# Fourier units of a hybrid GLA/FNet step: 388 columns in one product, added at eviction

## The chip, the core and the metric

One core of one Trainium2 chip runs the whole program. The metric is the device time of one execution in microseconds (us), as the median of several runs. A profile is one execution taken by the hardware profiler; its span runs from the first to the last instruction.

The engines are TensorE (PE, with its weight loads as PEld), VectorE (DVE), ScalarE (ACT), GpSimd (POOL) and SyncE (SP), which here issues nearly all DMA transfers. Each executes its own instructions in order; they meet at semaphores.

## The reference

One layer of a diffusion backbone, on 128 context and 256 latent tokens (T = 384 columns everywhere), with 2048 channels:

```
mod = silu(cond) @ w_ada + b_ada            # six shifts, scales and gates
h = rmsnorm(x) * (1 + sc1) + sh1
proj = h @ w_in                             # GLA q, k, v, output gate, decay factors, Fourier channels
o = bidirectional gated linear attention, normalised, times silu(gate)
f = real part of the 2-D DFT of the Fourier channels over (positions, group channels), 4 groups of 256
g_a, g_b = sigmoid(h @ w_gate + b_gate)
merged = g_a * (o @ w_br_gla) + g_b * (f @ w_br_four)
x = x + ga1 * rmsnorm(merged @ w_out)
x = x + ga2 * rmsnorm(swiglu_ffn(rmsnorm(x) * (1 + sc2) + sh2))
```

Everything is float32. The part that the change touches is `f @ w_br_four`, with its gate. The real DFT is symmetric over positions: with n positions only n/2 + 1 are computed, 65 for the context and 129 for the latent tokens, 194 in all (`HT`), once as a cosine part and once as a sine part. Their sum gives one half of the positions, their difference, read backwards, the other.

## The kernel before, in words

Channels lie on the 128 partitions and tokens along the columns. A float32 matrix is split into a high part (rounded to `float32r`, which TensorE takes in one pass) and a low part (what is left), and a product is three TensorE instructions: high by high, high weight by low data, low weight by high data (`gemm`, L253 to L260). The data are split once. The weights come from memory as slabs of 128 x 1024 and are split on the way.

The weights have one order, written out by hand (`srcs`, L147 to L188). `grab` (L244) takes the slab that is due and at once starts the preparation of a later one (`push`): a transfer into one of two `raw` buffers (L196, on SP's queue), for a slab of `w_br_four` a fold on VectorE (L205 and L206, a sum and a difference of halves), a cast to the high part on ScalarE (L224), and the subtraction of the low part on VectorE (L225). Three slabs are ready or being made while one is used; `whi` and `wlo` have four buffers each. A Fourier slab's cast and subtraction are put off until the unit's output has been written in program order (`hold`, `settle`). PE, ACT, DVE and POOL execute in the order of the program text (`manual_schedule`, L129).

The stages: the modulation of the first sub-layer with the value projection; query and key; the gates (32 projections) with the attention beside them; the Fourier projection (L888 to L904: eight projections, with the DFT over channels and positions beside them, `dft`, L822); the mixing stage (L958 to L986); the output projection (L1020 on); the FFN.

The mixing stage goes through `mix_order` (L155 to L158): O0, then seven rounds of one O product and two Fourier units (O1, unit 0, unit 1, O2, unit 2, unit 3, ...), then A0, unit 14, A1, unit 15, A2 to A15. An O product (`proj` with `gcol`, L926) uses two slabs of `w_in`, 48 products of 384 columns; its eviction is a SiLU on ScalarE (L931, after a table load), three transposes (L929), a product on VectorE (L932), a cast (L283) and a subtraction (L284). An A product uses one slab of `w_br_gla`. A Fourier unit (`four`, L935) uses one slab of `w_br_four`: for the cosine part `eT` and the sine part `dT` of the data it runs `gemm` over four blocks of 128 channels, 12 products of 194 columns each, and one Nyquist product (L943). Both parts accumulate side by side in one PSUM bank (`pf`, from the pool `psm`, three buffers). ScalarE copies the sine part to `d` (L946; tag `fd`, one buffer), VectorE writes sums and differences to `y` in four pieces (L950, L951) and multiplies by the gate (L954), SP writes `y` to memory (L955). `gate_of` (L909) loads the gates ahead and applies the sigmoid on ScalarE. A second PSUM pool, `pss` (tag "side", five buffers), holds transposes and the products beside the main ones.

The modulation of the later sub-layers (`ada_rest`, L519) is spread over the stages: a step is a 512 KB transfer (L525) and two operations on VectorE of 128 x 1024 (L528 for the first block, L530 for the others); after 16 of them come an empty step, a reduction on TensorE (L538) and, with the next half's first block, two transposes (L547) and small VectorE operations (L552 on). Half a projection, or an A product, is a chance for a step; `paced` (L271) uses the share `rate[0]` of the chances: 1.0 in the gate stage, 0.7 in the Fourier projection, 0.25 in the mixing stage, 0.15 from A0 on, 0.6 in the output projection.

Of the kernel before, what the change touches and what calls it, by code (L numbers as in the profile page):

```python
# [11 lines left out]
F32 = mybir.dt.float32  # L12
F32R = mybir.dt.float32r
# [7 lines left out]
P = 128  # L21
# [4 lines left out]
T = TC + TL  # L26
# [22 lines left out]
HT = HC + HL  # L49
# [47 lines left out]
def tile_step(ctx: ExitStack, tc: tile.TileContext, a, o):  # L97
    nc = tc.nc
    PE, ACT, DVE, POOL, SP = nc.tensor, nc.scalar, nc.vector, nc.gpsimd, nc.sync
# [3 lines left out]
    actp = ctx.enter_context(tc.tile_pool(name="actp", bufs=1))  # L103
# [129 lines left out]
    def settle():  # L233
        if half_done:
            half_done.pop()()

    def push(at=None, eng=DVE, hold=False):
        load()
        split(at, eng, hold)

    def take():
        return ready.pop(0)

    def grab(hold=False):  # L244
        w = take()
        push(hold=hold)
        return w
# [5 lines left out]
    def gemm(dst, w, x, kts, n=P, n0=0, k0=0, first=True, last=True):  # L253

        for k in range(kts):
            for j, (wi, xi) in enumerate(((0, 0), (0, 1), (1, 0))):
                PE.matmul(  # L257
                    dst, w[wi][:, k * n + n0 : k * n + n0 + P], x[xi][:, k0 + k, :],
                    start=first and k == 0 and j == 0, stop=last and k == kts - 1 and j == 2,
                )  # L260
# [21 lines left out]
    def split_act(hi, lo, src):  # L282
        ACT.copy(hi, src)  # L283
        DVE.tensor_sub(lo, src, hi.bitcast(F32))  # L284
# [29 lines left out]
    psm = ctx.enter_context(tc.tile_pool(name="psm", bufs=3, space=PSUM))  # L314
    pss = ctx.enter_context(tc.tile_pool(name="pss", bufs=5, space=PSUM))
    with ExitStack() as s:
# [89 lines left out]
        def xprod(u, kb, w):  # L406
            def mm():
                for j, (x_, w_) in enumerate(passes(w)):
                    PE.matmul(px, w_[:, u * P : (u + 1) * P], hT[x_][:, kb, :], start=j == 0, stop=j == 2)  # L409

            return mm, lambda dst=None: flush(xacc[u], kb == 0, dst)
# [92 lines left out]
        for t in range(3):  # L504
            vprod(KT - 1, prev[0], range(3), (t,))
            if t < XU:
                mm, fl = xprod(t, KT - 1, prev[1])
# [59 lines left out]
    rate = [1.0]  # L567
# [235 lines left out]
    with ExitStack() as s:  # L803
        pc = s.enter_context(tc.tile_pool(name="pc", bufs=1))
# [3 lines left out]
        SP.dma_start(cd, a["consts"][:, b0:NC])  # L808
        oT = alloc_r("B", "o")

        cl = actp.tile([P, 13 * HT], F32R, tag="C_lo", name="edT").rearrange("p (n t) -> p n t", t=HT)
        eT, dT = (cl[:, 0:4], cl[:, 4:8]), (cl[:, 8:12], pc.tile([P, 4, HT], F32R, name="dlo"))
        pnr = cl[:, 12]
        fs = {}
        nyq = pc.tile([P, 3, P], F32, name="nyq")
        POOL.memset(nyq, 0.0)
# [2 lines left out]
        wn = pc.tile([P, D], F32R, name="wn")  # L819
        done = [0]  # L820

        def dft():  # L822


            def left(dst, stat, m):

                for lat, base, n in ((0, C_CT - b0, HC), (1, C_LT - b0, HL)):
                    for k in range(1 + lat):
                        c0 = base + (m * (1 + lat) + k) * n
                        PE.matmul(  # L830
                            dst[:, HC * lat : HC * lat + n], stat(lat + k), cd[:, c0 : c0 + n],
                            start=k == 0, stop=k == lat,
                        )

            for g in range(4):
                while done[0] < 2 * g + 2:
                    yield
                yield
                xc = pc.tile([P, 3, 2, 2, P], F32, tag="xc", name="xc")
                for t in range(3):  # L840
                    px = pss.tile([P, 257], F32, tag="side", name="px")
                    ts = slice(t * P, (t + 1) * P)
                    e, d = fs[g][:, 0, ts], fs[g][:, 1, ts]
                    PE.matmul(px, d, cd[:, 129:386], start=True, stop=False)  # L844
                    PE.matmul(px[:, 0:129], e, cd[:, 0:129], start=False, stop=True)

                    for m, c0 in enumerate((0, 129)):
                        ACT.copy(xc[:, t, m], px[:, c0 : c0 + P].unsqueeze(1).to_broadcast([P, 2, P]))
                    ACT.copy(nyq[:, t, g : g + 65 : 32], px[:, 128:129].to_broadcast([P, 3]))
                yield  # L850
                off = (P - 32 * g) % P
                rot = xc.rearrange("p t m r c -> p t m (r c)")
                for m, x in enumerate((eT, dT)):
                    pp = pss.tile([P, HT], F32, tag="side", name="pp")
                    left(pp, lambda k: rot[:, k, m, off : off + P], m)
                    split_act(x[0][:, g, :], x[1][:, g, :], pp)
                yield
            pn = pss.tile([P, HT], F32, tag="side", name="pn")
            left(pn, lambda k: nyq[:, k, :], 0)
            ACT.copy(pnr, pn)  # L860
            DVE.tensor_sub(pnr[64:96], pn[64:96], pnr[64:96].bitcast(F32))
            yield

        def nyq_weights(h):

            n = D // 2
            wr = pc.tile([P, n], F32, tag="ws", name="wr")
            POOL.memset(wr, 0.0)
            for g in range(4):
                src = a["w_br_four"][8 * h : 8 * h + 8, 32 * g : 32 * g + 1, (2 * g + 1) * P : (2 * g + 2) * P]  # L870
                for j in range(3):
                    r = 32 * j + g
                    SP.dma_start(wr[r : r + 1, :].rearrange("p (i c) -> p i c", c=P), src.rearrange("i p c -> p i c"))
            yield
            w = wn[:, n * h : n * h + n]
            ACT.copy(w, wr)
            DVE.tensor_sub(w[32:64], wr[32:64], w[32:64].bitcast(F32))
            yield

        df = dft()  # L880

        def side():
# [4 lines left out]

        sd = side()  # L888
        nw = (u for h in range(2) for u in nyq_weights(h))
        rate[0] = 0.7  # L890
        for i in range(8):
            def fo(p, i=i):
                if i % 2 == 0:
# [40 lines left out]

        def four(i):  # L935

            pf = psm.tile([P, 512], F32, tag="mm", name="pf")
            p = pf[:, 0 : 2 * HT].rearrange("p (m t) -> p m t", m=2)
            w = grab(hold=True)
            for m, x in enumerate((eT, dT)):  # L940
                gemm(p[:, m, :], [v[:, 512 * m : 512 * m + 512] for v in w], x, 4, last=m == 1)
                if m == 0:
                    PE.matmul(p[:, 0, :], wn[0:96, i * P : (i + 1) * P], pnr[0:96], start=False, stop=True)  # L943
            g, _ = gates.pop(("b", i))
            d = pc.tile([P, HT], F32, tag="fd", name="fd")
            ACT.copy(d, p[:, 1, :])  # L946
            y = pc.tile([P, T], F32, tag="yb", name="y", bufs=4)
            for lo, n, base in ((0, TC, 0), (TC, TL, HC)):
                h = n // 2
                DVE.tensor_add(y[:, lo : lo + h], p[:, 0, base : base + h], d[:, base : base + h])  # L950
                DVE.tensor_sub(  # L951
                    y[:, lo + h : lo + n], p[:, 0, base + h : base : -1], d[:, base + h : base : -1],
                )
            DVE.tensor_mul(y, y, g)  # L954
            SP.dma_start(four_d[i], y)  # L955
            settle()

        rate[0] = 0.25  # L958
        mT, late = None, []
        for b, i in mix_order:  # L960
            if b == "o":
                if i == 1:
                    gate_of()
                proj(psm, hT, lambda p: gcol(p, i), sd)
                if i == 1:
                    gate_of()
                continue
            if b == "b":
                four(i)
            else:  # L970
                if mT is None:
                    mT = alloc_A()
                    rate[0] = 0.15
                p = psm.tile([P, T], F32, tag="mm", name="pmm")
                gemm(p, grab(hold=True), oT, 8)
                g, y = gates.pop((b, i))
                DVE.tensor_mul(g, g, p)
                DVE.tensor_add(y, y, g)
                settle()
                if late:  # L980
                    split_act(*late.pop())
                late.append((mT[0][:, i, :], mT[1][:, i, :], y))
                step(sd)
            gate_of()
# [6 lines left out]
    with ExitStack() as s:  # L991
# [30 lines left out]
        for i in range(KT):  # L1022
            p = psm.tile([P, T], F32, tag="mm", name="pmm")
            for g in range(2):
                w = grab()
# [93 lines left out]
        for k in range(KT + 1):  # L1119
# [6 lines left out]
            if k:  # L1126
                if k % 8 == 1:
                    hw = [take() for _ in range(HEAD)]
                for n, (j, m) in enumerate(((0, 0), (1, 0), (0, 1))):
                    for u in range(HEAD):  # L1130
                        PE.matmul(  # L1131
                            hp[u], hw[u][j][:, ((k - 1) % 8) * P : ((k - 1) % 8 + 1) * P], h2[m][:, k - 1, :],
                            start=k == 1 and n == 0, stop=k == KT and n == 2,
# [24 lines left out]
        for u in range(HEAD):  # L1158
            kind, c, j = ffn_order[u]
# [172 lines left out]
```

## Time and profile before

| | |
|---|---|
| runs before: median of 3 | 2057.03 us (2055.79 to 2059.26) |
| profiled execution, device time | 2056.04 us |
| its span | 2054.3 us |
| mean granted TensorE clock | 0.994 |
| Fourier products of 194 columns (`pf`, L257 and L943) | 400, from 605.6 to 711.6 us |

How to read the rows in what follows. A row of the timeline has the start in us from the start of the span, the duration in us, the engine, the line of the kernel, the operation, out<-in by the names in the program, partitions and columns, and in brackets how long the engine sat idle before it and for whom. A row of a group has the busy time in us and the mean in ns. A row of a stretch (A:B) has its length, then the busy time of PE, PEld, DVE, ACT and POOL with the number of instructions, the granted TensorE clock, the share of the DMA engines and GB/s. TensorE's products are pipelined, so their recorded durations overlap; the distance between two starts is what one costs.

### The profile page before, as it was taken

How to read it: one execution, taken by the hardware profiler on the slowest of the kernel's cores; microseconds unless marked ns; L12 is line 12 of the kernel's file. 1: busy time of each engine (PE TensorE's matmuls, PEld its weight loads, DVE VectorE, ACT ScalarE, POOL GpSimd, SP SyncE). 2: the span in 40 equal slices, each digit the busy share in tenths (PEclk: the TensorE clock that was granted, in tenths of full speed). 3: DMA queues.
4: the chain of work that ended last, by engine and by line, in shares of the span. 5: the costliest groups of instructions: out<-in, count | busy, mean ns of one | idle time of the engine just before them, and what ended most of it. 6: DMA issues, size and time to landing. Idle time of an engine off the chain costs nothing.

```text
span 2054.3 us, 30097 instructions
## 1 busy us (share of the span) xinstructions
PE 2024.7 (99%) x12214; PEld 1956.1 (95%) x12214; DVE 1274.9 (62%) x1663; ACT 770.1 (37%) x1143; POOL 45.4 (2%) x52
## 2 busy tenths in 40 slices
PE   8999999999999999999999999999999999999998
PEld 5779999999999999978999999999999999999996
DVE  5669787898667778867444555553545454544346
ACT  3233545453346544445333322222222322222234
POOL 0000000000000000022000000000000000000001
PEclk9999999999999999999999999999999999999998
DMA  9978677767646785532444444443444444433332
GB/s 387 354 261 274 206 238 230 240 222 259 202 158 209 257 282 183 187 113 93 154 144 152 146 144 154 144 146 125 150 144 147 151 144 148 148 125 124 123 133 83
DMA packets 112563, 373.94 MB, mean 182 GB/s; under 512 B 13860, under 2 KB 32484, under 8 KB 108328
## 3 DMA queue, kind: packets, MB, share of 16 engines
q1 hardware_dynamic: 111560, 370.84, 52.8%
q8 instruction: 96, 1.57, 0.3%
q10 hardware_dynamic: 864, 1.18, 0.2%
q14 instruction: 43, 0.35, 0.1%
HBM read 358.34 MB, written 13.63 MB: 181 GB/s over the span
## 4 chain that ended last, share of the span: by engine, by line
PE 96%; DVE 2%; DMA 1%; ACT 1%; issue 0%; SPq 0%; DVEq 0%; ACTq 0%
PE pmm L257 66%; PE pdn L257 18%; PE pv L391 3%; PE pf L257 2%; PE pgm L374 1%; PE px L409 1%; DVE yE L1227 0%; PE po L603 0%; PE pmm L1131 0%; DMA Clo<-in_xT 0%; PE pr L538 0%; DMA slab<-in_w_ada 0%; DVE z L1090 0%; PE dl L603 0%; PE px L844 0%
## 5 line engine op out<-in xcount | busy, mean ns | idle before, releaser
L257 PE MATMUL pmm<-A_hi,whi 128*128 128x384 f32 x2480 | 832.6, 336 | 0.0
L257 PE MATMUL pmm<-A_hi,wlo 128*128 128x384 f32 x2480 | 828.9, 334 | 0.0
L257 PE MATMUL pmm<-A_lo,whi 128*128 128x384 f32 x2480 | 828.8, 334 | 0.0
L225 DVE TENSOR_TENSOR wlo<-raw,whi 128x1024 fp32r<-128x1024 f32 x433 | 529.0, 1223 | 433.8 <-ACT whi L224 432.9
L224 ACT CAST whi<-raw 128x1024 fp32r<-128x1024 f32 x436 | 457.7, 1050 | 587.4 <-PE pmm L257 223.2
L257 PEld LDWEIGHTS pmm<-A_hi,whi 128*128 128x128 f32 x2480 | 465.6, 188 | 3.4 <-issue 1.8
L257 PEld LDWEIGHTS pmm<-A_lo,whi 128*128 128x128 f32 x2480 | 465.7, 188 | 0.2
L257 PEld LDWEIGHTS pmm<-A_hi,wlo 128*128 128x128 f32 x2480 | 465.6, 188 | 0.0
L530 DVE SCALAR_TENSOR_TENSOR adacc<-adaw,spad,adacc 128x1024 f32<-128x1024 f32 x240 | 296.9, 1278 | 0.6 <-DMA adaw<-in_w_ada 0.3
L257 PE MATMUL pdn<-hid_hi,whi 128*128 128x384 f32 x704 | 235.2, 334 | 0.0
L257 PE MATMUL pdn<-hid_hi,wlo 128*128 128x384 f32 x704 | 235.1, 334 | 0.0
L257 PE MATMUL pdn<-hid_lo,whi 128*128 128x384 f32 x704 | 235.1, 334 | 0.0
L257 PEld LDWEIGHTS pdn<-hid_hi,whi 128*128 128x128 f32 x704 | 132.2, 188 | 0.4 <-issue 0.4
L257 PEld LDWEIGHTS pdn<-hid_lo,whi 128*128 128x128 f32 x704 | 132.2, 188 | 0.0
L257 PEld LDWEIGHTS pdn<-hid_hi,wlo 128*128 128x128 f32 x704 | 132.2, 188 | 0.0
L283 ACT CAST hid_hi<-hfE 128x384 fp32r<-128x384 f32 x44 | 22.6, 513 | 161.6 <-DVE hfE L1154 161.6
L1154 DVE TENSOR_TENSOR hfE<-sg,pmm 128x384 f32<-128x384 f32 x44 | 24.4, 555 | 82.2 <-PE pmm L257 81.6
L1146 ACT ACTIVATE sg<-pmm 128x384 f32<-128x384 f32 x44 | 21.6, 492 | 133.5 <-PE pmm L257 133.5
L1171 DVE TENSOR_TENSOR Blo<-Blo,pdn 128x384 f32<-128x384 f32 x72 | 39.5, 553 | 46.6 <-PE pdn L257 46.6
L1171 DVE TENSOR_TENSOR Bhi<-Bhi,pdn 128x384 f32<-128x384 f32 x72 | 39.0, 549 | 34.0 <-PE pdn L257 34.0
L257 PE MATMUL pmm<-o_hi,whi 128*128 128x384 f32 x128 | 42.8, 335 | 0.0
L257 PE MATMUL pmm<-o_lo,whi 128*128 128x384 f32 x128 | 42.8, 334 | 0.0
(301 smaller groups left out, 1556.9 us busy)
## 6 DMA issues: line engine op xcount, KB each, us to landing
adaw<-in_w_ada SPq DMA_DIRECT2D x128, 512.0 KB
raw<-in_w_g SPq DMA_DIRECT2D x88, 512.0 KB
raw<-in_w_u SPq DMA_DIRECT2D x88, 512.0 KB
raw<-in_w_d SPq DMA_DIRECT2D x88, 512.0 KB
slab<-in_w_ada SPq DMA_DIRECT2D x32, 1024.0 KB
raw<-in_w_gate SPq DMA_DIRECT2D x64, 512.0 KB
raw<-in_w_in SPq DMA_DIRECT2D x44, 512.0 KB
raw<-in_w_out SPq DMA_DIRECT2D x32, 512.0 KB
```

The costliest lines, as they stand in the source:

```text
L224: ACT.copy(hi, raw)
L225: eng.tensor_sub(lo, raw, hi.bitcast(F32))
L257: PE.matmul(dst, w[wi][:, k * n + n0 : k * n + n0 + P], x[xi][:, k0 + k, :], start=first and k == 0 and j == 0, stop=last and k == kts - 1 ...
L283: ACT.copy(hi, src)
L374: PE.matmul(pgv[q : q + 32, :], spad[:, k, :], slab[k // (KT // 2)][:, k % (KT // 2), :], start=k < 4, stop=k >= KT - 4,)
L391: PE.matmul(pv[2 * t + g], hT[x_][:, kb, t * P : (t + 1) * P], w_[:, g * 512 : (g + 1) * 512], start=kb == 0 and j == 0, stop=kb == KT - 1 ...
L409: PE.matmul(px, w_[:, u * P : (u + 1) * P], hT[x_][:, kb, :], start=j == 0, stop=j == 2)
L530: DVE.scalar_tensor_tensor(acc[:, c, :], w, spad[:, k, c : c + 1], acc[:, c, :], op0=ALU.mult, op1=ALU.add,)
L1146: ACT.activation(sgs[j], p, AF.Silu)
L1154: DVE.tensor_mul(hf, sgs.pop(j), p)
L1171: DVE.tensor_add(acc(k), acc(k), p)
```

## The change

In `four` the three products of a block become two. The high and the low part of a block's data now lie next to one another (`parts`, in place of four separate groups), 388 columns; the high weight takes both in one product, into two halves of a PSUM bank, and the low weight takes the high part, 194 columns, into the first half. So a unit has 17 products in place of 25. Cosine and sine part have a bank each, the second from `pss`. At eviction ScalarE copies the second half of each bank to `d`, now of twice the size, and VectorE adds the first half: two copies in place of one, and two additions that were not there. The four output pieces then read `d` alone. The rates of the modulation steps change from 0.7 to 1.0 in the Fourier projection and from 0.25 to 0.1 in the mixing stage.

```diff
-        cl = actp.tile([P, 13 * HT], F32R, tag="C_lo", name="edT").rearrange("p (n t) -> p n t", t=HT)
-        eT, dT = (cl[:, 0:4], cl[:, 4:8]), (cl[:, 8:12], pc.tile([P, 4, HT], F32R, name="dlo"))
-        pnr = cl[:, 12]
+        cl = actp.tile([P, 15 * HT], F32R, tag="C_lo", name="edT").rearrange("p (n t) -> p n t", t=HT)
+        d3 = pc.tile([P, 2, HT], F32R, name="d3")
+        parts = [cl[:, 2 * n : 2 * n + 2] for n in range(7)] + [d3]
+        eT, dT = parts[:4], parts[4:]
+        pnr = cl[:, 14]
...
-                    split_act(x[0][:, g, :], x[1][:, g, :], pp)
+                    split_act(x[g][:, 0], x[g][:, 1], pp)
...
-        rate[0] = 0.7
+        rate[0] = 1.0
...
-            pf = psm.tile([P, 512], F32, tag="mm", name="pf")
-            p = pf[:, 0 : 2 * HT].rearrange("p (m t) -> p m t", m=2)
             w = grab(hold=True)
+            d = pc.tile([P, 2, HT], F32, tag="fd", name="fd")
+            y = pc.tile([P, T], F32, tag="yb", name="y", bufs=4)
             for m, x in enumerate((eT, dT)):
-                gemm(p[:, m, :], [v[:, 512 * m : 512 * m + 512] for v in w], x, 4, last=m == 1)
+                pf = (pss if m else psm).tile([P, 512], F32, tag="side" if m else "mm", name="pf")
+                for k in range(4):
+                    c = slice(512 * m + k * P, 512 * m + (k + 1) * P)
+                    PE.matmul(pf[:, 0 : 2 * HT], w[0][:, c], x[k], start=k == 0, stop=False)
+                    PE.matmul(pf[:, 0:HT], w[1][:, c], x[k][:, 0], start=False, stop=m == 1 and k == 3)
                 if m == 0:
-                    PE.matmul(p[:, 0, :], wn[0:96, i * P : (i + 1) * P], pnr[0:96], start=False, stop=True)
+                    PE.matmul(pf[:, 0:HT], wn[0:96, i * P : (i + 1) * P], pnr[0:96], start=False, stop=True)
+                ACT.copy(d[:, m], pf[:, HT : 2 * HT])
+                DVE.tensor_add(d[:, m], d[:, m], pf[:, 0:HT])
             g, _ = gates.pop(("b", i))
-            d = pc.tile([P, HT], F32, tag="fd", name="fd")
-            ACT.copy(d, p[:, 1, :])
-            y = pc.tile([P, T], F32, tag="yb", name="y", bufs=4)
             for lo, n, base in ((0, TC, 0), (TC, TL, HC)):
                 h = n // 2
-                DVE.tensor_add(y[:, lo : lo + h], p[:, 0, base : base + h], d[:, base : base + h])
+                DVE.tensor_add(y[:, lo : lo + h], d[:, 0, base : base + h], d[:, 1, base : base + h])
                 DVE.tensor_sub(
-                    y[:, lo + h : lo + n], p[:, 0, base + h : base : -1], d[:, base + h : base : -1],
+                    y[:, lo + h : lo + n], d[:, 0, base + h : base : -1], d[:, 1, base + h : base : -1],
                 )
             DVE.tensor_mul(y, y, g)
             SP.dma_start(four_d[i], y)
             settle()
 
-        rate[0] = 0.25
+        rate[0] = 0.1
```

## The prediction, made before the result was known

> **What bounds the kernel now.** I read the page first, then busy time by stage, then the timeline of the Fourier stage engine by engine.
>
> ```profile
> span 2054.3 us, 30097 instructions
> PE 2024.7 (99%) x12214; PEld 1956.1 (95%) x12214; DVE 1274.9 (62%) x1663; ACT 770.1 (37%) x1143; POOL 45.4 (2%) x52
> PE 96%; DVE 2%; DMA 1%; ACT 1%; issue 0%; SPq 0%; DVEq 0%; ACTq 0%
> 228.00:490.00 262.00, 262.00 (x1699) 255.69 (x1691) 222.17 (x286) 125.31 (x218) 1.88 (x6) 1.00 0.72 235
> 520.00:605.00 85.00, 83.66 (x505) 82.45 (x504) 55.40 (x60) 33.28 (x70) 0.96 (x1) 1.00 0.57 190
> PE px L844 <- issue: 1.3, 1, 1.3
> ```
>
> The chain is TensorE nearly everywhere, so work taken from TensorE shortens the kernel, as long as nothing else is close behind it. (The last line is the whole list of TensorE's waits from 520 to 780 us: none is for a weight.) In the stage of the change (605 to 712 us) something is. Follow one round of it: O4, units 4 and 5, O5. Weights are prepared three ahead: a transfer (L196), for Fourier weights a fold on VectorE (L205, L206), a cast on ScalarE (L224), a subtraction on VectorE (L225).
>
> ```profile
> 627.48 0.68 DVE L206 TENSOR_TENSOR ws<-raw 128x512 f32<-128x512 f32 x1
> 628.19 0.33 SPq L196 DMA_DIRECT2D raw<-in_w_in  x1
> 631.92 1.05 ACT L224 CAST whi<-ws 128x1024 fp32r<-128x1024 f32 x1 [2.25 <-DVE ws L206]
> 633.00 1.23 DVE L225 TENSOR_TENSOR wlo<-ws,whi 128x1024 fp32r<-128x1024 f32 x1 [1.12 <-ACT whi L224]
> 633.61 1.05 ACT L224 CAST whi<-raw 128x1024 fp32r<-128x1024 f32 x1 [0.64 <-DMA raw<-in_w_in]
> 635.97 0.49 ACT L931 ACTIVATE gs<-pmm 128x384 f32<-128x384 f32 x1
> 636.50 0.61 DVE L932 SCALAR_TENSOR_TENSOR gs<-gs,gnorm,pt 128x384 f32<-128x384 f32 x1 [0.58 <-ACT gs L931]
> 637.14 0.51 ACT L283 CAST o_hi<-gs 128x384 fp32r<-128x384 f32 x1 [0.68 <-DVE gs L932]
> 637.56 1.05 ACT L224 CAST whi<-raw 128x1024 fp32r<-128x1024 f32 x1
> 638.64 1.23 DVE L225 TENSOR_TENSOR wlo<-raw,whi 128x1024 fp32r<-128x1024 f32 x1 [0.40 <-ACT whi L224]
> 639.79 0.22 DVE L950 TENSOR_TENSOR y<-pf,fd 128x64 f32<-128x64 f32 x1
> 641.64 0.68 DVE L206 TENSOR_TENSOR ws<-raw 128x512 f32<-128x512 f32 x1
> 636.90 0.28 PE L257 MATMUL pf<-edT,whi 128*128 128x194 f32 x1
> 608.42 0.39 PE L257 MATMUL pf<-edT,whi 128*128 128x194 f32 x2
> ```
>
> The end of unit 4's fold (627.48 + 0.68 = 628.16) frees the buffer of the next transfer (628.19); its data are there at 633.61; cast, table load, SiLU, product, cast, the next weight's cast and its subtraction follow; then unit 4's output (639.79), then unit 6's fold. **From fold to fold 641.64 - 627.48 = 14.16 us, and not one step in it waits for TensorE.** It is a loop of its own, through SP, DMA, ScalarE and VectorE. A round of TensorE is hardly longer: unit 1 starts at 608.42, unit 5, two rounds on, at 636.90, 14.24 us a round. Unit 5's weight was ready at 633.00 + 1.23 = 634.23; this lead of 2.7 us shrinks as soon as TensorE's round gets shorter than the loop.
>
> **What the change does, part by part.**
>
> ```profile
> 611.10 0.27 PE L257 MATMUL pf<-edT,wlo 128*128 128x194 f32 x1
> 611.21 0.36 PE L257 MATMUL pmm<-A_hi,whi 128*128 128x384 f32 x1
> 611.41 0.34 PE L257 MATMUL pmm<-A_lo,whi 128*128 128x384 f32 x1
> 611.58 0.34 PE L257 MATMUL pmm<-A_hi,wlo 128*128 128x384 f32 x1
> ```
>
> *TensorE.* A unit has 25 products of 194 columns from 608.42 to 611.21: 0.1116 us each. Products of 384 columns follow one another in 0.17 us, 0.45 ns a column; at that rate 194 columns would take 0.087. So the narrow ones are held by something else at 0.111, the loading of weights. A pair of 388 and 194 columns costs 388 x 0.45 = 0.175 plus 0.111: 0.286 where three products cost 0.335. Eight pairs and the Nyquist product: 8 x 0.286 + 0.111 = 2.40 instead of 2.79 us. Saving 0.39 a unit, 16 units **6.2 us**, if TensorE stays the bound. Bounds: with the narrow product hidden down to its columns 0.262 a pair (9.3 us); with the 0.20 that the first wide product took behind narrow ones, 0.20 + 0.111 (3.1 us). I take 0.286, as the narrow products' row is this very shape.
>
> The Trainium skill ("TensorE: Matmul & The Clock Gate", Step-by-step: what each phase is for) says that a 64-deep window pulls weight loads ahead of running products. By that rule the pair costs the 0.262. The trace speaks against: a train of narrow products stays at 0.111, so no store of loads is built up.
>
> *VectorE.* Per unit two additions of 194 columns are new; the four output operations read two SBUF operands instead of one in PSUM, which I count at nothing.
>
> ```profile
> L284 DVE TENSOR_TENSOR dlo<-pp,edT 128x194 fp32r<-128x194 f32 x4 | 1.4, 357 | 0.9 <-ACT edT L283 0.9
> L946 ACT COPY fd<-pf x16: 308/322/325, 609.9 to 715.2; 128x194 f32<-128x194 f32 x16
> 642.70 0.28 DVE L951 TENSOR_TENSOR y<-pf,fd 128x128 f32<-128x128 f32 x1
> 643.02 0.56 DVE L954 TENSOR_TENSOR y<-y,gate 128x384 f32<-128x384 f32 x1
> ```
>
> The nearest row has the same shape and one operand in PSUM: 0.357. Neighbours that don't depend on each other overlap by 0.08 (638.64 + 1.23 against 639.79), a dependent one starts 0.04 behind the end (642.70 + 0.28 against 643.02). First addition 0.28, second 0.36 + 0.04: **0.68 a unit**. Lower bound 0.56, upper 0.80. They stand between the subtraction at 638.64 and the output at 639.79, so in the loop. The additional ScalarE copy (0.32) lies beside that subtraction and costs nothing there; without that cover, 0.3 a unit. The second part's accumulator takes a buffer of the five-deep pool, which here serves transposes; hidden. Two waits are added: the first addition waits for its copy, with the outputs and the next fold behind it on VectorE; and the copies wait for the single `fd` buffer until the unit before is put out, with a sigmoid and the next cast behind them. VectorE's multiply and fold (0.56 and 1.2 us) cover the second. SP's write of the output comes later too, but the transfers behind it wait for the fold anyway.
>
> The Trainium skill ("VectorE: DVE Perf Modes", Rules for kernel authors) advises few VectorE operations rather than fewer semaphores. That speaks against this edit; by whole rows two additions cost 0.71, by the spacings 0.68.
>
> *Modulation steps.* A full step is one 512 KB transfer on SP's queue and two operations:
>
> ```profile
> 607.77 2.47 DVE L530 SCALAR_TENSOR_TENSOR adacc<-adaw,spad,adacc 128x1024 f32<-128x1024 f32 x2
> 662.70 1.07 PE L538 MATMUL pr<-adacc,selr 128*32 128x256 f32 x16
> 694.72 0.23 DVE L552 COPY mods<-ptm 128x8 f32<-128x8 f32 x2
> 695.29 1.41 DVE L528 TENSOR_SCALAR adacc<-adaw,spad 128x1024 f32<-128x1024 f32 x2
> ```
>
> By the rates 11 of 16 chances were used in the Fourier projection and 4 in the stage; now it is 16 and 1. Five steps more in the projection put 5 x 2.4 = 12 us on VectorE and 2.6 MB on DMA: VectorE from 55.4 to 67 of 85 us (80%), where the gate stage ran at 222 of 262 (85%) with TensorE never idle. Hidden; the cover fails if transfers come late. But the reduction (1.07) and its two transposes (0.2) move there too, **+1.3 us** while TensorE is the bound there; in the stage they stood where TensorE was about to wait anyway. In the stage the four steps were a multiply-add at 607.77, off the loop, an empty one, the reduction, and 1.9 us from 694.72 to 696.62. Now 0.1 a chance adds up to one multiply-add, at the eleventh, in O5.
>
> *The sum, in the loop's terms*, for the weight of unit 13, with the waits that take up delay:
>
> ```profile
> 616.96 0.69 DVE L205 TENSOR_TENSOR ws<-raw 128x512 f32<-128x512 f32 x1 [0.73 <-DMA raw<-in_w_br_four]
> 662.11 1.05 ACT L224 CAST whi<-raw 128x1024 fp32r<-128x1024 f32 x1 [0.48 <-DMA raw<-in_w_in]
> 675.98 1.06 ACT L224 CAST whi<-raw 128x1024 fp32r<-128x1024 f32 x1
> 689.53 1.23 DVE L225 TENSOR_TENSOR wlo<-ws,whi 128x1024 fp32r<-128x1024 f32 x1 [1.12 <-ACT whi L224]
> 695.28 0.39 PE L257 MATMUL pf<-edT,whi 128*128 128x194 f32 x2
> 701.80 1.23 DVE L225 TENSOR_TENSOR wlo<-raw,whi 128x1024 fp32r<-128x1024 f32 x1 [1.51 <-ACT whi L224]
> 706.89 1.23 DVE L225 TENSOR_TENSOR wlo<-ws,whi 128x1024 fp32r<-128x1024 f32 x1
> 709.21 0.25 PE L257 MATMUL pf<-edT,whi 128*128 128x194 f32 x1
> ```
>
> Later start 1.3; units 0 and 1, 1.36 less the wait of 0.73: 0.6; units 2, 4, 6, 8 and 10, 5 x 0.68 = 3.4; unit 11, whose additions delay the next fold, 0.7; the odd units' additions where a transfer's wait no longer covers them (0.48 at 662.11, none at 675.98) 0.2 + 0.7, some 1.0; the step in O5, 2.4 less two waits like the 0.40 and 0.58 of the round above, 1.4. Together 8.4. The weight was ready at 689.53 + 1.23 = 690.76, 4.5 ahead of 695.28, so unit 13 starts 3.9 us later than now, and TensorE's 5 us saved by then are spent on waiting. On to unit 15: 8.4, less 1.9 for the step that is gone from 695, plus 1.4 for units 12 and 13, less the wait of 1.5 at 701.80, is 6.4; its weight was ready at 706.89 + 1.23 = 708.12, 1.1 ahead of 709.21: 5.3 later, less its own 0.4: **+4.9 us**. Behind it come wide products only, TensorE is the bound again, and what is lost stays lost. Against the profiled execution's 2056.04 (its span and 1.7 around it) that is 2060.9; the median shown is 1.0 above, so 2061.9. With additions of 0.56 and the odd units hidden it is 2.0 less; with 0.80 and the step whole, 2.0 more: 2059.9 to 2063.9.
>
> **The rivals.**
>
> *TensorE stays the bound.* For it: 99% busy, and no wait of TensorE on a weight in this stage. Then 6.2 us are won: 2050.8. It decides if the loop gives way by 0.7 us a round, for instance if the transfer (628.19 to 633.61, 5.4 us, mixed with smaller ones) arrives sooner once these start later. Against: with the transfer out of the way the folds and casts of the odd unit (631.92, 633.00) are right behind it. Half way lies 2055.
>
> *Weight loads run further ahead* and TensorE is the bound: 9.3 us, 2047.8. That is the first page's rule.
>
> *The projection stage can't carry 16 steps.* If half of the 12 us came through there, 6 more: 2068. Against: the gate stage's share above.
>
> *It does not do what it says*: the products and columns are counted in the code, so only the pair's price is open, and in a stage bound by the loop that price changes nothing.
>
> **How the numbers follow.** The loop binds as summed (2059.9 to 2063.9, likeliest 2061.9): 0.60. It binds in part (2053 to 2059.9): 0.13. TensorE stays the bound: 0.15, with loads further ahead 0.03. Projection stage too: 0.09. A measurement of this kernel tells about 0.2% from no change, 4.1 us: 2052.9 to 2061.1. Faster 0.18; same 0.13 and four tenths of the first case, 0.37; slower 0.36 + 0.09 = 0.45. The range goes from 2050.5, so that the full gain is in it, to 2064.5; the likeliest case's own stands above.
>
> **What would show it.** Right: TensorE waits for `wlo` L225 or `whi` L224 of odd units from about unit 3 on; fold to fold about 14.9 us; units of 2.40 us where TensorE doesn't wait; the projection stage about 1.3 us longer, with no waits. Wrong: no such waits, and rounds of 13.5 us; or fold to fold still 14.2, with the additions beside a wait that I have not seen.

## The result, and the profile after

| | before | after |
|---|---|---|
| median (range), 6 runs each | 2057.41 us (2055.79 to 2059.26) | 2068.99 us (2065.33 to 2071.20) |
| ratio, 95% interval | | 1.0054 [1.0043, 1.0065] |
| profiled execution, its span | 2056.04, 2054.3 us | 2067.78, 2066.0 us |

The change costs 11.6 us, where 4.9 were forecast. The stages begin, in TensorE's timeline, with the first product of the Fourier projection, of O0, of unit 0, of A2 and of the output projection. In the kernel before these start at 506.02, 584.30, 605.57, 711.98 and 770.24 us; in the changed kernel:

```profile
506.08 0.33 PE L257 MATMUL pmm<-A_hi,whi 128*128 128x384 f32 x1
590.93 0.33 PE L257 MATMUL pmm<-A_hi,whi 128*128 128x384 f32 x1
612.19 0.42 PE L948 MATMUL pf<-edT,whi 128*128 128x388 f32 x1
721.45 0.36 PE L257 MATMUL pmm<-o_hi,whi 128*128 128x384 f32 x1
781.95 0.33 PE L257 MATMUL pmm<-A_hi,whi 128*128 128x384 f32 x1
```

The differences of neighbours, with the kernels of the experiments below in the same way (O0 and O1 together take 21.26 us in all of them, and from the output projection to the end it is 1284.0 to 1284.1, but 1286.8 in `gate_nyq_ahead`):

| kernel | projection | units 0 to 15, with A0 and A1 | A2 to A15 | median |
|---|---|---|---|---|
| before | 78.28 | 106.41 | 58.26 | 2057.4 |
| after | 84.85 | 109.26 | 60.50 | 2069.0 |
| after_again | 85.43 | 109.75 | 59.08 | 2068.7 |
| products_only | 78.57 | 110.07 | 58.27 | 2062.0 |
| rates_only | 85.71 | 104.99 | 58.26 | 2062.4 |
| no_additions | 85.25 | 105.06 | 59.45 | 2061.5 |
| nyq_on_pool | 78.02 | 109.20 | 58.27 | 2060.5 |
| pool_gate_nyq | 78.02 | 112.33 | 59.07 | 2063.6 |
| gate_nyq_ahead | 78.02 | 112.00 | 60.06 | 2065.9 |
| pool_extra | 78.02 | 119.56 | 58.57 | 2071.0 |
| before_nyq_pool | 76.55 | 106.41 | 58.26 | 2054.5 |
| rates_nyq_pool | 78.02 | 105.62 | 58.34 | 2055.0 |

So the 11.7 us of span are 6.57 in the projection, 2.85 in the mixing stage and 2.24 in the A products. (What lies ahead of the projection differs by up to 2.7 us between executions, whatever the kernel; stages are therefore compared by length.) The chain by engine, from the profile page of the changed kernel:

```profile
PE 87%; DVE 6%; ACT 2%; DMA 2%; issue 2%; SPq 1%; POOL 0%; ACTq 0%; DVEq 0%; POOLq 0%
```

The list of TensorE's waits there from 500 to 800 us, which had one entry of 1.3 us before:

```profile
PE pf L949 <- DVE wlo L225: 6.0, 8, 0.8
PE px L847 <- issue: 3.3, 1, 3.3
PE pmm L257 <- DVE gate L984: 2.0, 1, 2.0
PE px L847 <- DVE fs L901: 1.1, 1, 1.1
PE pmm L257 <- DVE wlo L225: 0.7, 1, 0.7
```

TensorE's share of the chain falls from 96% to 87%, and the chain now runs through VectorE, a DMA and SP's queue. The first line of the list is the mixing stage, with eight waits for a low part of a Fourier weight, and so is the last, with one in an O product. The second and fourth are the projection, the third an A product.

**The mixing stage** goes as forecast. The unit's pairs, and the round from fold to fold:

```profile
626.04 0.36 PE L948 MATMUL pf<-edT,whi 128*128 128x388 f32 x1
626.23 0.25 PE L949 MATMUL pf<-edT,wlo 128*128 128x194 f32 x1
626.33 0.36 PE L948 MATMUL pf<-edT,whi 128*128 128x388 f32 x1
...
635.20 0.68 DVE L206 TENSOR_TENSOR ws<-raw 128x512 f32<-128x512 f32 x1
642.72 0.36 PE L949 MATMUL pf<-edT,wlo 128*128 128x194 f32 x1 [0.71 <-DVE wlo L225]
647.49 0.62 DVE L953 TENSOR_TENSOR fd<-fd,pf 128x194 f32<-128x194 f32 x2
650.02 0.68 DVE L206 TENSOR_TENSOR ws<-raw 128x512 f32<-128x512 f32 x1
```

A pair takes 626.33 - 626.04 = 0.29 us. The loop takes 650.02 - 635.20 = 14.82 us instead of 14.16, with the two additions (647.49) ahead of the outputs. TensorE meets the late low part for the first time in unit 5 (642.72).

**The projection** is where the forecast failed. The timeline of SP, VectorE, ScalarE and TensorE in the changed kernel, and the granted clock of the stretch after the gap (TensorE's columns: busy time and instructions first, the clock third from the end):

```profile
513.60 8.06 SPq L876 DMA_DIRECT2D wr<-in_w_br_four  x12
521.78 1.27 SPq L525 DMA_DIRECT2D adaw<-in_w_ada  x1
523.16 0.37 SPq L196 DMA_DIRECT2D raw<-in_w_in  x1
526.13 2.48 DVE L530 SCALAR_TENSOR_TENSOR adacc<-adaw,spad,adacc 128x1024 f32<-128x1024 f32 x2 [8.72 <-DMA adaw<-in_w_ada]
527.44 1.05 ACT L224 CAST whi<-raw 128x1024 fp32r<-128x1024 f32 x1 [11.29 <-DVE adacc L530]
526.71 0.34 PE L257 MATMUL pmm<-A_hi,wlo 128*128 128x384 f32 x1
530.31 0.67 PE L847 MATMUL px<-cd,fs 128*128 128x257 f32 x2 [3.26 <-issue]
533.09 0.67 PE L257 MATMUL pmm<-A_hi,whi 128*128 128x384 f32 x1
535.14 0.33 PE L257 MATMUL pmm<-A_hi,whi 128*128 128x384 f32 x1
553.43 0.70 PE L847 MATMUL px<-cd,fs 128*128 128x257 f32 x2 [1.14 <-DVE fs L901]
```

```profile
530.00:535.00 5.00, 4.69 (x18) 4.21 (x19) 4.90 (x6) 3.22 (x11) 0.51 (x1) 0.67 0.95 330
```

SP spends 8 us on twelve small transfers for the Nyquist weights (L876), 0.67 us each. Behind them, at 521.78, stands a modulation slab that the new rate puts there, and only behind that, at 523.16, the next weight slab. VectorE has been idle for 8.72 us when the modulation slab arrives, and works on it first. ScalarE's cast of the weight slab comes at 527.44. VectorE's subtraction for that slab, and behind it the sums `fs` (L901) that TensorE's DFT (L847) reads, follow. The same place before:

```profile
513.33 8.06 SPq L873 DMA_DIRECT2D wr<-in_w_br_four  x12
521.49 2.10 SPq L196 DMA_DIRECT2D raw<-in_w_in  x2
523.64 0.90 SPq L525 DMA_DIRECT2D adaw<-in_w_ada  x2
526.65 0.34 PE L257 MATMUL pmm<-A_hi,wlo 128*128 128x384 f32 x1
528.33 0.67 PE L844 MATMUL px<-cd,fs 128*128 128x257 f32 x2 [1.34 <-issue]
530.42 0.42 PE L257 MATMUL pmm<-A_hi,whi 128*128 128x384 f32 x1
```

There the weights were issued ahead of the modulation slabs. Does the cast wait for VectorE's step, as its bracket says, or for its own slab? At 527.44 both are possible. In `rates_only` (experiment 2), with the same order on SP's queue, the two lie apart:

```profile
529.31 1.04 ACT L224 CAST whi<-raw 128x1024 fp32r<-128x1024 f32 x1 [11.90 <-DMA raw<-in_w_in]
530.39 1.23 DVE L225 TENSOR_TENSOR wlo<-raw,whi 128x1024 fp32r<-128x1024 f32 x1 [1.02 <-ACT whi L224]
```

VectorE is done with its step there and waits 1.02 us for the cast, which waits for its slab. So in that run what comes last is the weight slab that was issued behind the modulation slab, not VectorE's work.

From the rows of the kernel before and the changed one: the gap is 530.31 - 526.71 = 3.6 us instead of 1.7 (+1.9). The DFT behind it takes 533.09 - 530.31 = 2.8 instead of 2.1, and the next six products 535.14 - 533.09 = 2.05 where six at the usual 0.17 take 1.0, while the clock is down (+1.7 together). A second gap, of 1.1 us at 553.43, is new and follows the second block of Nyquist transfers. The moved reduction I count with the forecast's 1.3 (experiments 7 and 10 differ by 1.5). Together 6.0 of 6.57.

### The profile page after: what moved, and what is told of

The parts are those of the page before. It is cut to its first block, busy times and chain, and to the rows that moved or that the text cites. A ratio compares the mean times of both kernels' runs of the same rounds, so it can differ in the third digit from the quotient of the medians.

```text
span 2066.0 us, 29890 instructions
## 1 busy us (share of the span) xinstructions
PE 2024.4 (98%) x12086; PEld 1951.4 (94%) x12086; DVE 1285.1 (62%) x1695; ACT 773.4 (37%) x1159; POOL 45.4 (2%) x52
## 4 chain that ended last, share of the span: by engine, by line
PE 87%; DVE 6%; ACT 2%; DMA 2%; issue 2%; SPq 1%; POOL 0%; ACTq 0%; DVEq 0%; POOLq 0%
PE pmm L257 60%; PE pdn L257 18%; PE pv L391 3%; PE pgm L374 1%; ACT whi L224 1%; PE px L409 1%; DVE wlo L225 1%; DMA raw<-in_w_br_gla 1%; SPq L876 1%; DMA raw<-in_w_in 1%; DVE yE L1234 0%; PE po L603 0%; DVE adacc L530 0%; PE pr L538 0%; DMA Clo<-in_xT 0%
```

## The experiments

Theory A, formed from these rows: two independent costs. The additions lie in VectorE's loop, so the saving on TensorE is spent on waiting for weights; and the five further steps cost the projection through the place of their transfers on SP's queue, behind the Nyquist block. The rivals: the steps cost it by VectorE's work or by bandwidth, whatever the queue; and the mixing stage loses by something else than the additions.

**1 and 2. Half of the change each.** `products_only` is the changed kernel with the old rates (0.7 and 0.25); `rates_only` is the kernel before with the new ones (1.0 and 0.1).

```diff
-        rate[0] = 1.0        (products_only)
+        rate[0] = 0.7
-        rate[0] = 0.1
+        rate[0] = 0.25
```

> The new products and eviction with the old rates (0.7 and 0.25). Theory A: of the 11.6 us, 6.6 come from the Fourier projection, where a modulation step at every chance makes VectorE wait for a transfer that stands behind twelve small ones on SP's queue; only 2.9 come from the mixing stage, whose loop through VectorE and ScalarE binds, and 2.2 from the A products. Then the projection stage is 78.3 us as before, the mixing stage 3 to 4.5 us longer than before, and the whole 3 to 6 us above before, 2060.5 to 2063.5. Rival B: the products and additions are what costs, and fewer steps in the mixing stage help; then putting the steps back makes it slower than the changed kernel, 2069 or more.

> The kernel before with the new rates (1.0 and 0.1), products and eviction as they were. Theory A: the projection stage is some 6.6 us longer (84.8 us), the mixing stage 1.3 us shorter since its reduction has moved, the A products the same: 4 to 6.6 us above before, 2061.5 to 2064. Rival B: the steps are hidden behind TensorE, at most 1.3 us move from one stage to the other: within 2 us of before.

Measured: `products_only` 2062.04 us (2059.30 to 2064.53), 1.0018 [1.0009, 1.0027]; `rates_only` 2062.44 (2061.31 to 2064.69), 1.0023 [1.0014, 1.0032], against 2057.58 for the kernel before in the same session. By the table the products alone cost 3.7 us in the mixing stage and 0.3 in the projection; the rates alone cost 7.4 in the projection and give 1.4 back in the mixing stage. Each half is a loss by itself. Both costs are where theory A has them.

**3. The changed kernel without the two additions.**

```diff
-                ACT.copy(d[:, m], pf[:, HT : 2 * HT])
-                DVE.tensor_add(d[:, m], d[:, m], pf[:, 0:HT])
+                ACT.copy(d[:, m], pf[:, 0:HT])
```

> The changed kernel without the two additions of a unit: ScalarE copies the first half of each accumulator, so the product of the high weight with the low data is computed but left out of the result. Theory A: the loop loses 0.65 us a round, so fold to fold goes from 14.8 to about 14.2 us and the mixing stage gets 3.5 to 5.5 us shorter; the projection stage stays at 84.8 us. 4 to 7 us below the changed kernel. Rival C, the additional ScalarE copies or the second accumulator bind and not the additions: less than 1 us below the changed kernel.

Measured: 2061.51 us (2060.16 to 2064.03), 1.0021 [1.0012, 1.0030], 7.5 below the changed kernel. The mixing stage takes 105.06 us instead of 109.26; the profiled executions differ by 4.8 in all (2061.2 against 2066.0 of span), and the rest of the 7.5 they don't show. Its loop:

```profile
635.01 0.68 DVE L206 TENSOR_TENSOR ws<-raw 128x512 f32<-128x512 f32 x1
...
663.86 0.69 DVE L206 TENSOR_TENSOR ws<-raw 128x512 f32<-128x512 f32 x1
```

Two rounds later, so 28.85 / 2 = 14.4 us a round: 0.4 of the 0.66 are gone, where all of it was expected. What holds the rest, the second ScalarE copy for instance, no run separates. Yet 105.06 is what `rates_only` needs with the old products (104.99). So even with the additions at no cost the eight products fewer a unit win nothing: TensorE waits instead, five times and 3.1 us in all for the low part of a Fourier weight, where `rates_only` has no wait in this stage. That the loop and not TensorE sets this stage is shown.

**4. The Nyquist transfers on GpSimd's queue**, in the changed kernel.

```diff
-                    SP.dma_start(wr[r
+                    POOL.dma_start(wr[r
```

> The changed kernel with the 24 small transfers of the Nyquist rows issued by GpSimd instead of SP. Theory A: the modulation slabs no longer stand behind 8 us of small transfers, VectorE's wait of 8.7 us for one goes, and the projection stage is 79.6 to 81 us (before 78.3, and 1.3 for the reduction that moved): 4 to 5 us below the changed kernel. Rival D, five more steps are simply too much for VectorE in that stage: the wait goes but the stage stays above 83.5 us, and the time falls by less than 1.5 us.

Measured: 2060.47 us (2058.60 to 2062.19), 1.0012 [1.0004, 1.0021], 8.5 below the changed kernel. The projection takes 78.02 us with all sixteen steps in it. SP's and GpSimd's timelines (the first eight transfers of the first block, and the whole second block), and the whole list of TensorE's waits from 500 to 790 us:

```profile
512.60 0.38 SPq L525 DMA_DIRECT2D adaw<-in_w_ada  x1
...
513.99 4.28 POOL L876 DMA_DIRECT2D wr<-in_w_br_four  x8 [0.31 <-POOL wr L871]
...
531.01 6.13 POOL L876 DMA_DIRECT2D wr<-in_w_br_four  x12 [0.29 <-POOL wr L871]
```

```profile
PE pf L949 <- DVE wlo L225: 6.0, 8, 0.8
PE pmm L257 <- DVE wlo L225: 0.7, 1, 0.7
```

The slab goes out at 512.60, not at 521.78, and no wait is left in the projection. VectorE does the same work there as in the changed kernel, so it was the queue: sixteen steps fit into that stage, as forecast, if the transfers aren't held back. The gain is more than expected: the gap that the kernel before had there is gone too, and by the profiles 2.2 us come from the A products (58.27 instead of 60.50).

**5 and 6. The gate's product on GpSimd as well, and a third raw buffer.** With the projection mended, I took VectorE's last operation of a unit out of the loop; then I added a buffer and one more slab under way (the constants' buffer, from O1 to A0).

```diff
-            DVE.tensor_mul(y, y, g)
+            POOL.tensor_mul(y, y, g)
...
+            if raw is None and third[0] is not None:
+                third[0] += 1
+                if third[0] % 3 == 1:
+                    raw = fold_in[0].tile([P, NC - C_CR], F32, tag="cd", name="raw3")[:, 0:G]
...
+                    third[0] = 0
+                    load()
```

> The changed kernel with the small Nyquist transfers on GpSimd's queue (as in nyq_on_pool) and, new, the multiplication by the gate on GpSimd, so that VectorE loses one operation of 0.47 us in every unit. Theory A: the mixing stage is bound by the loop from fold to fold; the multiplication of the first unit of a round leaves it, that of the second only shortens the path beside the transfer, so fold to fold goes from 14.8 to about 14.3 us and the stage from 109.2 to 105 to 107 us, 2 to 4 us below nyq_on_pool. Rival E: VectorE's work alone binds; both multiplications count, 13.9 us a round, and the stage falls below 104 us, 5 us or more. Rival F: the loop is not the cause of the stage's length: within 1 us of nyq_on_pool.

> As pool_gate_nyq, and in the mixing stage one slab more is on its way: a third buffer for raw slabs, in the place of constants that are no longer read by then. Theory A: with the transfer out of the loop both multiplications count: fold to fold about 13.9 us, close to TensorE's 13.6, so the lead at the start of the stage lasts, the stage takes 101 to 104 us, and the whole lies 2 to 5 us below pool_gate_nyq and below the kernel before. Rival E, transfers are not in the loop: within 1 us of pool_gate_nyq.

Measured: 2063.58 us (2061.70 to 2065.74), 1.0027 [1.0017, 1.0036], and 2065.90 (2063.63 to 2067.75), 1.0035 [1.0022, 1.0047]. All my theories missed: the first was to win and lost 3.1 us against experiment 4, with the mixing stage at 112.33 us instead of 109.20. Its timeline, GpSimd's row first:

```profile
643.08 1.35 POOL L961 TENSOR_TENSOR y<-y,gate 128x384 f32<-128x384 f32 x1 [9.97 <-DVE y L958]
643.46 1.51 DVE L206 TENSOR_TENSOR ws<-raw 128x512 f32<-128x512 f32 x1
...
646.49 1.86 POOL L961 TENSOR_TENSOR y<-y,gate 128x384 f32<-128x384 f32 x1 [2.07 <-DVE y L958]
647.53 1.38 DVE L205 TENSOR_TENSOR ws<-raw 128x512 f32<-128x512 f32 x1
```

A fold that takes 0.69 us alone takes 1.51 and 1.38 beside the product. Both times it ends 0.5 to 0.6 us after GpSimd's end (643.08 + 1.35 = 644.43 against 644.97; 648.35 against 648.91): it stood until GpSimd was done. VectorE saves 0.56 and loses 0.7 to 0.8. The third buffer left the stage nearly as it was (112.00). Of the 2.7 us more from the output projection on, 2.1 lie in one wait of TensorE, at a weight in GpSimd's care, that takes 0.7 in experiment 4's kernel:

```profile
PE pst L297 <- POOL wlo L231: 2.8, 1, 2.8
```

Why that weight comes later there I did not follow up, and the buffer was not tried without GpSimd's product.

**7 and 8. The kernel before with the Nyquist transfers on GpSimd's queue, and the changed kernel once more.** The edit of the first is that of experiment 4; the second has none and asks whether the A products' 2.2 us belong to the kernel.

> The kernel before with the small Nyquist transfers on GpSimd's queue, nothing else. Theory A: the block on SP's queue costs the kernel before too, in the one wait of TensorE of 1.3 us in the projection stage; it goes, 1 to 2 us below before. Rival: it costs only where a step is taken at every chance; within 0.5 us.

> The changed kernel itself, a second profiled execution. The projection stage at 84.9 us and the mixing stage at 109.3 us should come again within 1 us. Open is whether the A products' 2.2 us (60.5 instead of 58.3) belong to the kernel or to that one execution: if to the kernel, 59.5 or more again; if to one late transfer, about 58.3.

Measured: `before_nyq_pool` 2054.49 us (2053.93 to 2055.94), 0.9985 [0.9976, 0.9994], about 3 us below the kernel before. It beats both kernels. Its projection takes 76.55 instead of 78.28 us, 1.7 less; where the rest of the 3 comes from the one profile doesn't show. `after_again`: 2068.68 us in its one execution, with 85.43 and 109.75 us in the two stages, and 59.08 in the A products. So the first two repeat within 0.6 us, while the last shows 0.8 instead of 2.2. In the first execution the wait was for a slab that came late:

```profile
745.65 1.05 ACT L224 CAST whi<-raw 128x1024 fp32r<-128x1024 f32 x1 [5.37 <-DMA raw<-in_w_br_gla]
```

It is gone with experiment 4 (58.27), but what makes it come and go is open.

**9. A product on GpSimd that nothing needs.** Experiment 4's kernel, with VectorE's own work unchanged:

```diff
             DVE.tensor_mul(y, y, g)
+            POOL.tensor_mul(g, g, y)
             SP.dma_start(four_d[i], y)
```

> The kernel with the Nyquist transfers on GpSimd's queue, VectorE's gate product kept as it is, and one further product on GpSimd behind it in each Fourier unit (the gate times the finished output, into the gate's buffer, which nothing reads any more). The product is extra work that no result depends on. Theory P (a GpSimd product and a VectorE operation with both inputs in the on-chip memory shut each other out: in the run with the product moved to GpSimd the second fold took 1.51 us instead of 0.68 beside it): VectorE, which sets the loop, loses 0.7 to 1.5 us in each round although none of its own operations changed; folds or low parts beside the product show 1.4 us or more, the mixing stage takes 112 to 117 us instead of 109.2, and the kernel 2063 to 2068. Theory L (that run was slow because the gated output came later and was written out later, or because the product's chain was longer): output and its write are where they were, so nothing changes: 2059.5 to 2061.5, the stage 109 to 110.

Measured: 2070.96 us (2070.23 to 2072.11), 1.0056 [1.0039, 1.0073], 10.5 over experiment 4. The mixing stage takes 119.56 us: theory P, and more than it asked for. Two pairs of rows, and the groups of the folds from 612 to 712 us:

```profile
648.48 1.33 POOL L962 TENSOR_TENSOR gate<-gate,y 128x384 f32<-128x384 f32 x1 [10.57 <-ACT fd L952]
648.86 1.50 DVE L206 TENSOR_TENSOR ws<-raw 128x512 f32<-128x512 f32 x1
...
652.48 1.85 POOL L962 TENSOR_TENSOR gate<-gate,y 128x384 f32<-128x384 f32 x1 [2.67 <-DVE y L961]
653.51 1.38 DVE L205 TENSOR_TENSOR ws<-raw 128x512 f32<-128x512 f32 x1
```

```profile
L206 DVE TENSOR_TENSOR ws<-raw 128x512 f32<-128x512 f32 x12 | 13.1, 1090 | 0.0
L205 DVE TENSOR_TENSOR ws<-raw 128x512 f32<-128x512 f32 x12 | 12.4, 1032 | 0.2
```

The same groups in experiment 4's kernel:

```profile
L205 DVE TENSOR_TENSOR ws<-raw 128x512 f32<-128x512 f32 x14 | 9.6, 687 | 0.2
L206 DVE TENSOR_TENSOR ws<-raw 128x512 f32<-128x512 f32 x14 | 9.6, 684 | 0.0
```

A mean fold pays 0.35 to 0.41 us, 12 x 0.75 = 9.0 us in this window, and the stage grows by 10.4. The output, its write and every VectorE instruction were the same, and the profile shows no engine that waits for the extra product, so a late output isn't the cause. The same slow folds explain experiment 5.

**10. The new rates with the old products, and the queue mended.**

> The kernel before with its products, the new rates of the modulation steps (all sixteen in the projection) and the Nyquist transfers on GpSimd's queue. Theory A (the rates cost the projection stage only through the queue, and the products cost the mixing stage 4 us by the additions): the projection stage takes about 78.0 us, the mixing stage about 105.0, the rest as before, so the kernel takes 2053.5 to 2056.5, the same as the kernel before with only the queue changed (2054.5): the reduction's 1.3 us only moved from one stage to the other. Theory F (sixteen steps are too many for that stage even so): projection over 80 us and the kernel 2057 to 2061.

Measured: 2055.03 us (2054.21 to 2057.23), 0.9986 [0.9977, 0.9995]; projection 78.02, mixing stage 105.62. Theory A: against experiment 7 the move of the steps costs 1.5 in one stage and gives 0.8 in the other; the net 0.7 no run tells from zero. And against experiment 4, which differs by the products alone, the products cost 109.20 - 105.62 = 3.6 us in the stage and 2060.47 - 2055.03 = 5.4 in the medians.

## Why the prediction was wrong

The direction was right, and the likeliest mechanism, but the time lies above the range: 2069.0, where the range ends at 2064.5 and the likeliest time was 2061.9.

*TensorE's pair*, forecast 0.286 us: 0.29 (626.04, 626.33); units 0 and 1 together 4.90 us (612.19 to 617.09), forecast 4.80, before 5.64 (605.57 to 611.21), so 0.37 less a unit. Right. The rule of the Trainium skill that the prediction names ("TensorE: Matmul & The Clock Gate", Step-by-step: what each phase is for), weight loads pulled ahead, would by the prediction's working have made 0.262, and the trace doesn't show that: the narrow product starts 0.19 us after the wide one, and the next wide one 0.10 later.

*VectorE's additions*, forecast 0.68 us a unit: they start at 632.67, the output pieces behind them at 633.32, so 0.65. *The loop*, forecast "about 14.9": 14.82. *Waits for the low part*: there, though from unit 5 and not 3. *The mixing stage*, forecast 4.9 - 1.3 = +3.6: +2.85 (+3.34 in the second execution). All right in mechanism, and right in size to within 0.8 us.

*The step that failed* is "Five steps more in the projection put 5 x 2.4 = 12 us on VectorE and 2.6 MB on DMA ... Hidden". The projection grew by 6.57 us instead of 1.3. The 12 us of VectorE are hidden indeed: in experiment 4 they are all there, and no wait is. The prediction says itself that "the cover fails if transfers come late", and doesn't ask what would make them late. What I left out is the queue that the moved steps' transfers go through: at the new rate a modulation slab stands behind the Nyquist block and ahead of a weight slab, and the DFT waits for what that weight slab holds up (a gap of 3.6 us instead of 1.7). I had counted SP's part as bytes and set a share of busy time in another stage (85% in the gate stage) against it. But the gate stage has no block of twelve small transfers in SP's way. The one wait in my own list, 1.3 us at `px` L844, was the sign that at this place something already came last, and I took it as proof that nothing was close.

*The rival "projection stage can't carry 16 steps"* named 2068 at a chance of 0.09. Its time fits, its mechanism (work on VectorE that comes through) doesn't, so that hit is luck.

*The A products*, forecast 0: +2.24 and +0.82. Not explained.

So of the miss, 2069.0 - 2061.9 = 7.1 us: 5.3 are the projection (6.57 - 1.3), 0.8 to 2.2 the A products, less 0.8 or 0.3 in the mixing stage.

## What to carry to other kernels

A step that is moved to another stage brings its transfer, and what decides is what stands ahead of that transfer on its queue at the new place, and what then stands behind it: read the queue's own timeline there, and price each small transfer by its issue time. A wait already in the list, however short, marks a place where something comes last, and what is put ahead of it can show in full. Before one engine's work is cut, ask whether another loop is as long as its round: here 5.9 us of TensorE's time (16 x 0.37) bought nothing, even with the additions taken away.

## What the runs showed of the hardware

*VectorE and GpSimd shut each other out* for operations whose two inputs both lie in the on-chip memory: 0.69 us became 1.38 to 1.51 (experiments 5 and 9). It goes by who starts first: in experiment 9 GpSimd's second product, recorded from 652.48, takes 1.85 us beside a VectorE subtraction that began before it and runs from 652.26 to 653.48. The fold recorded from 653.51 then stands until that product ends at 654.33, and itself ends at 654.89. The Trainium skill ("SBUF — State Buffer", Who interferes with whom) says that a VectorE instruction with two operands in that memory contends with a GpSimd instruction that reads it, and that the later one is blocked until the earlier one ends. The rows agree.

*TensorE's clock after a gap.* After 3.6 us without products the clock was lower until about 535 us (0.67 over the stretch from 530 to 535), which cost about 1.7 us more. After the 1.7 us gap of the kernel before the clock stayed at 1.00. Experiment 4's kernel shows it again, far from the change:

```profile
913.00:917.00 4.00, 0.31 (x1) 0.00 (x0) 3.56 (x7) 0.66 (x2) 2.93 (x4) 1.00 0.38 131
917.00:920.00 3.00, 2.89 (x5) 1.71 (x6) 2.97 (x5) 0.55 (x2) 2.92 (x3) 0.51 0.02 5
```

So the gap of 3.6 us cost about half as much again. A long wait isn't the only way to a lower clock: in the kernel before, at this second place, the clock is 0.66 over 908 to 910 us and 0.50 over 910 to 913, although the one wait of TensorE ahead is 0.71 us; between 907 and 910 it runs 18 products of a single column. The Trainium skill ("TensorE: Matmul & The Clock Gate", What's actually happening) gives a window of about 3.4 us, idle or busy, for either change of the clock. The rows behind the two gaps agree for the one that falls; that it would not fall at 3 us no run here shows.

*Small transfers* cost the issuing queue 8.06 / 12 = 0.67 us each on SP and 6.13 / 12 = 0.51 on GpSimd, and whatever stands behind them waits for that time.
